# Another order of kept output blocks, the norm's squares in order, and value products in 64 columns, in a two-layer RG-LRU and attention kernel

## The chip, the cores and the metric

The kernel runs on one core of one Trainium2 chip. The metric is the device time of one execution in microseconds. The core's engines work side by side, each through its own queue in order: TensorE (PE in the profile, its weight loads PEld), VectorE (DVE), ScalarE (ACT), GpSimd (POOL) and SyncE (SP). POOL and SP do little but issue DMA transfers here. SBUF is the on-chip memory, PSUM the buffers that TensorE writes.

## What is computed

Two residual layers over one sequence of 1024 positions and 1024 channels, then a norm. The first mixes with a gated linear recurrence (width 1536, 12 blocks), the second with causal attention of 16 heads of 64 whose logits carry a forgetting term.

```python
def lru_mixer(h, ...):
    u = h @ w_in
    xb, gate = u[..., :1536], u[..., 1536:]
    xc = causal_depthwise_conv(xb, conv_w, conv_b)
    r = sigmoid(block_diag_linear(xc, wa, ba))
    i = sigmoid(block_diag_linear(xc, wx, bx))
    log_a = -8.0 * r * softplus(-a_param)
    a = exp(log_a)
    bterm = sqrt(-expm1(2.0 * log_a)) * (i * xc)
    hs = scan of h = a * h + bterm
    return (hs * silu(gate)) @ w_out

def fox_mixer(h, w_in, b_f, w_out):
    q, k, v, gate, f_logit = parts of h @ w_in
    cum = cumsum(log_sigmoid(f_logit + b_f))
    logits = q @ k.T / 8 + cum_q - cum_k, causal
    o = softmax(logits) @ v
    return (o * silu(gate)) @ w_out

x = x + lru_mixer(rms_norm(x), ...)
x = x + fox_mixer(rms_norm(x), ...)
out = rms_norm(x)
```

## The kernel before

Activations lie with the channels on the partitions, in two halves of 512 positions. Every product of the projections is made of two parts of each operand (`hi`, and `lo` = the rest), as three matmuls in a rounded 32-bit type: hi x hi, lo x hi, hi x lo (`gemm_steps`, line 128). `weights` (122) loads a weight block through a ring of tag `wf`, ScalarE makes `wh` and VectorE or GpSimd `wl`.

A scheduler places the instructions of each engine ahead of time by its own model of their durations. `tc.issue_after(i)` puts what stands in its block behind instruction `i` in the queue of `i`'s engine. All matmuls keep the order in which the program writes them, through `run` (853).

*First layer.* `split_x` and `square_x` (250, 261) make the two parts and the squares of x for one half; `square_x` adds seven of the eight squares into `acc` and keeps the last apart, so that `norm_row` (276) sums two tiles with matmuls against ones. The squares rotate through four buffers `sq`. `norm_row(0)` stands behind `square_x(1)`, which writes the same four buffers. `softplus` (213) works out constants of the recurrence; `conv(n)` (294), `gates`, `recur` and `outputs` follow for each of the 12 blocks.

*Between the layers* (lines 497 to 530) the last part of the output projection is added to x, x goes to DRAM as `x1d`, and `squares` and `rms_row` make the norm for each half: one tile of sums and, because of `wait`, the last square as a second tile; `inv_rms` (151) multiplies every tile with a column of ones, for four groups of 128 positions.

*Attention.* For each head, `maxima(hd, c)` (762) makes the scores `S` of four blocks of 128 queries in half c, VectorE masks them and takes the maximum, ScalarE the exponential. The weights become two f16 parts (`pp`: high in slot 0, low in slot 1) and a transposing DMA on SP turns them into `pT`. `weigh(hd, c)` (808) multiplies them with `v`, also two f16 parts of 64 columns each, side by side: one matmul against high and low of the weights for each block j of 128 keys, 8 in the first half of the positions and 16 in the second. O then holds in 64 partitions what the high part of v gives and in the other 64 what the low part gives, and lines 829 and 830 add the two. The parts of `v` lie in the order high of head 0, low of head 0, low of head 1, high of head 1.

`run` interleaves by hand: in an order string "1" is a step of the next scores, "0" a step of the products and "." a unit of the fill, six matmuls of the projections for later pairs of heads. `ORDER` (29) holds the strings for the first and the second half, `LAST` those of heads 12 on.

*Output.* From head 12 on the fill holds `partial` (912): for each of 8 blocks `db` of output channels and each half c, x1d is loaded by POOL, the product of the first six pairs of heads (`ops`, 18 matmuls in three steps) is added on VectorE (924) and the sum goes back to x1d by POOL (926). The order is (0, 0), (1, 0), (0, 1), (1, 1), (2, 0), (2, 1), (3, 0), (3, 1) and so on, as (db, c). Tiles come from a ring of two, tag `R`. Some blocks of half 0 are kept on chip instead (`kept`, line 919); their places come from `home` (902): two places in a buffer of tag `sg`, used until then for the gate of head pair 6, and four in the buffer `T0` of the keys, used until the scores of head 14 are done. `residual` (932) fetches the blocks that were not kept, on SP, into `U0` and the places that are left. `turned` (957) then transposes x, adds the last two pairs' products and does the final norm.

Of the kernel before, what the change touches and what calls it, by code (L numbers as in the profile page):

```python
# [19 lines left out]
P = 128  # L20
# [5 lines left out]
HD = 64  # L26
EPS = 1e-6
GROUP = 2
ORDER = "1.1..1.1..00", "1.1.1.1...0000"
LAST = "1..1..1..1..0.0", "1..1.1..1..0..0.0.0"  # L30
NEG = -1e30
PSUM = bass.MemoryType.PSUM
# [8 lines left out]
def trunk(ctx: ExitStack, tc: tile.TileContext, xt, w0, wg, wo0, pc, gn, gf, w1, wv, wf, bf, wo1, out):  # L41
# [17 lines left out]
    def matmul(*args, **kw):  # L59
        pe[0] = nc.tensor.matmul(*args, **kw)  # L60
        return pe[0]
# [126 lines left out]
    with ExitStack() as l0:  # L188
# [12 lines left out]
        def long(tag, dtype=F32, bufs=1):  # L201
            return tmp.tile([P, SEQ], dtype, tag=tag, name=tag, bufs=bufs)
# [54 lines left out]

        acc = long("m2")
        sq = [z[:, cs] for z in (long("th"), long("ti")) for cs in halves]

        def square_x(h):
            to = acc[:, halves[h]]
            sums[h].append(to)
            for k in range(KT):
                z = sq[k % 4] if k else to
                nc.scalar.activation(z, xs[h][k], AF.Square)
                if k == KT - 1:
                    sums[h].append(z)
                elif k:
                    nc.vector.tensor_tensor(to, to, z, ALU.add)  # L270
                yield
# [4 lines left out]
        def norm_row(h):  # L276

            row = ps.tile([P, HALF], F32, tag="O", name="rsrow")
            for i, sq_ in enumerate(sums[h]):
                matmul(row, onesf, sq_, start=i == 0, stop=i == len(sums[h]) - 1)  # L280
            r_ = rs[:, halves[h]]
            nc.scalar.activation(r_, row, AF.Sqrt, bias=epst, scale=1.0 / SEQ)
            return nc.vector.reciprocal(r_, r_)

        for _ in zip(split_x(0), square_x(0)):
            pass
# [122 lines left out]
        for n in range(NB):  # L409
            wu = first[0] if n == 0 else list(weights(w0[n]))  # L410
            if n == 1:
                ups = both = [ps.tile([P, HALF], F32, tag="g", name="ups") for h in range(2)]
            else:
                ups = two_banks("ups")
                both = [ups.rearrange("p a b -> p (a b)")]
                ups = [ups[:, h] for h in range(2)]
            product(ups[0], 0, wu)
            if n == 0:
                gps = held[0] = two_banks("gps")
                product(gps[:, 0], 0, first[1])  # L420
                for _ in zip(split_x(1), square_x(1)):
                    pass
                done = norm_row(0)
            else:
                gates(n - 1)
                if n > 1:
                    with tc.issue_after(state[n - 1]["last"].ins):
                        outputs(n - 2)
            product(ups[1], 1, wu)
            if n == 0:  # L430
                product(gps[:, 1], 1, first[1])
                norm_row(1)
                with tc.issue_after(done.ins):
                    softplus()
            conv(n, both)
            if n % 2 and n > 1:
                fill = itertools.chain(fill, project_out((n - 3) // 2))
            take(fill, 4)
            if n > 3:
                with tc.issue_after(state[n - 1]["last"].ins):  # L440
                    take(vsquares, 4)
            if n > 1:
                wn = list(weights(w0[NB + n - 1]))
                gps = held[n - 1] = two_banks("gps")
                for h in range(2):
                    product(gps[:, h], h, wn)
            if n:
                drain(silu(state[n - 1], held.pop(n - 1)))

                with tc.issue_after(state[n]["tap"].ins):  # L450
                    recur(n - 1)
            take(fill, 4)
# [45 lines left out]
        for h, cs in enumerate(halves):  # L498
            y = [tuple(z[:, cs] for z in p) for p in ys[-2:]]
            hT[h] = [pair() for k in range(KT)]  # L500
            parts = split_x(h, 1)
            sums = []
            for d0 in range(0, KT, 4):
                pts = []
                for db in range(d0, d0 + 4):
                    if db % 2 == 0:
                        two = ps.tile([P, 2, HALF], F32, tag="S", name="ops")
                    pts.append(two[:, db % 2])
                    mm3(pts[-1], wl[db][0], y[0], True, False)
                for db, o in enumerate(pts, d0):  # L510
                    mm3(o, wl[db][1], y[1], False, True)
                    x = xs[h][db]
                    nc.vector.tensor_tensor(x, x, o, ALU.add)  # L513
                    nc.sync.dma_start(x1d[h, :, db], x)
                    next(parts)
                    squares(
                        sums,
                        x,
                        lambda: nrm.tile([P, HALF], F32, tag="sq" if db else "ss", name="sq", bufs=2),
                        wait=db == KT - 1,  # L520
                    )
            rms_row(sums, rs1[h], rms1[h])
            if h == 0:
                value_bounds()
            nc.vector.tensor_tensor(
                rv[:, :, 4 * h : 4 * h + 4],
                rms1[h].unsqueeze(1).to_broadcast([P, 4, 4]),
                scale_v.unsqueeze(2).to_broadcast([P, 4, 4]),
                ALU.mult,
            )  # L530
# [7 lines left out]
    with ExitStack() as l1:  # L538
# [269 lines left out]
        def weigh(hd, c, sub=slice(0, HALF)):  # L808

            pair, s = hd // 2, hd % 2  # L810
            V, turned_ = Vs[pair], pT[c]
            if s == 0:
                yos[pair, c] = at.tile([P, HALF], F32, tag="yo", name="yo", bufs=2)
            yo = yos[pair, c][:, sub]
            begin, end = c * HALF + sub.start, c * HALF + sub.stop
            O = ps.tile([P, HALF], F32, tag="O", name="O")[:, : end - begin]
            nj = end // P
            for j in range(nj):
                v = V[j][:, 2 * s : 2 * s + 2].rearrange("p a d -> p (a d)")
                q = max(begin, j * P)  # L820
                for t in range(2):
                    p = turned_[:, j, t, q - c * HALF : end - c * HALF]
                    matmul(O[:, q - begin :], v, p, start=j == t == 0, stop=j == nj - 1 and t == 1)
                if j % 2 and j < nj - 1:
                    yield

            r0, r1 = s * HD, (1 - s) * HD
            to, one = yo[r0 : r0 + HD], unit_v[:, hd // 4 : hd // 4 + 1]
            nc.scalar.activation(to, O[r1 : r1 + HD], AF.Copy, scale=one[r1 : r1 + HD])
            nc.vector.scalar_tensor_tensor(to, O[r0 : r0 + HD], one[r0 : r0 + HD], to, ALU.mult, ALU.add)  # L830
            yield
# [69 lines left out]

        def home(db):

            if db == 3:
                two = at.tile([P, 2, HALF], F32, tag="sg", name="x3")
                homes[3], homes[2] = two[:, 0], two[:, 1]
            elif db == 5:
                four = tu.tile([P, 4, HALF], F32, tag="T0", name="x4")
                homes.update((4 + i, four[:, i]) for i in range(4))
            return homes[db]  # L910

        def partial(todo):

            for db, c in todo:
                split_out(db)
                if c if db < 2 else not c:
                    split_out(db + 1)

                kept = c == 0 and db in (3, 5, 6, 7)
                x = home(db) if kept else rpool.tile([P, HALF], F32, tag="R", name="xp")  # L920
                nc.gpsimd.dma_start(x, x1d[c, :, db])
                pt = ps.tile([P, HALF], F32, tag="g", name="ops1")
                yield from gemm_steps(pt, zip(wo[db], [y1[c][pair] for pair in range(6)]))
                nc.vector.tensor_tensor(x, x, pt, ALU.add)
                if not kept:
                    nc.gpsimd.dma_start(x1d[c, :, db], x)
# [5 lines left out]
        def residual(c, q):  # L932

            cs = slice(q * 256, (q + 1) * 256)
            if c == q == 0:
                two = tu.tile([P, 2, HALF], F32, tag="U0", name="x0")
                homes[0], homes[1] = two[:, 0], two[:, 1]
                for d in (0, 1, 2, 4):
                    fetch(homes[d], x1d[c, :, d])
            if c == 0:  # L940
                return [homes[d][:, cs] for d in range(KT)]
# [111 lines left out]
        for hd in range(HEADS):  # L1053
# [21 lines left out]
                    )  # L1075
            elif pair < 6:
                fill = chain(g_units(pair + 1), kq_units(pair + 2, ((1, (0,)),)))
            first, second = LAST if hd > 11 else ORDER
            if hd == HEADS - 1:
                first = "1..1.0.1.0.1..."  # L1080
            side = chain(pieces(hd + 1, 0, 0), pieces(hd + 1, 0, 1)) if hd else iter(())
# [105 lines left out]
```

## Time and profile before

| what | value |
|---|---|
| median of 3 runs | 1081.56 us (1079.12 to 1083.71) |
| the profiled execution | 1079.6 us |
| its span in the profile | 1077.8 us |
| mean granted TensorE clock | 0.995 |
| DMA moved | 142.55 MB |

The profile shows one execution. Busy times are per engine; a matmul's time is from its first column to its last result, so that successive matmuls overlap, and the distance between their starts tells what they take in a row. "f32" in a shape stands for four-byte elements, also the rounded type; "128*64" before a matmul's shape would be 128 active rows and 64 active columns of the array. A bracket at the end of a row of the order of time is the idle time of the engine before it and what ended it. Rows that an argument needs stand with it in the prediction.

### The profile page before, as it was taken

How to read it: one execution, taken by the hardware profiler on the slowest of the kernel's cores; microseconds unless marked ns; L12 is line 12 of the kernel's file. 1: busy time of each engine (PE TensorE's matmuls, PEld its weight loads, DVE VectorE, ACT ScalarE, POOL GpSimd, SP SyncE). 2: the span in 40 equal slices, each digit the busy share in tenths (PEclk: the TensorE clock that was granted, in tenths of full speed). 3: DMA queues.
4: the chain of work that ended last, by engine and by line, in shares of the span. 5: the costliest groups of instructions: out<-in, count | busy, mean ns of one | idle time of the engine just before them, and what ended most of it. 6: DMA issues, size and time to landing. Idle time of an engine off the chain costs nothing. (4 is left out here: it accounts for less than half of the span.)

```text
span 1077.8 us, 14962 instructions
## 1 busy us (share of the span) xinstructions
PE 1048.0 (97%) x5100; PEld 843.7 (78%) x5100; DVE 782.1 (73%) x1444; ACT 621.6 (58%) x1082; POOL 113.2 (11%) x91
## 2 busy tenths in 40 slices
PE   9999999999999999999999999999999999997997
PEld 7788888888888887797777797767977779765776
DVE  7889657766776589947878848788488866774665
ACT  8488453655465564745757636566466655653454
POOL 1322021202220210030000000000000000011200
PEclk9999999999999999999999999999999999998999
DMA  7111211222122112535878957899578885988994
GB/s 251 60 43 50 64 59 54 64 69 64 54 70 68 49 54 69 158 94 134 157 174 192 176 135 155 179 190 191 139 153 188 174 191 131 226 210 225 224 193 157
DMA packets 218508, 142.55 MB, mean 132 GB/s; under 512 B 161792, under 2 KB 178688, under 8 KB 218432
## 3 DMA queue, kind: packets, MB, share of 16 engines
q1 hardware_dynamic: 216032, 133.74, 52.3%
q0 software_dynamic: 2400, 7.87, 2.4%
q8 instruction: 40, 0.66, 0.3%
q14 instruction: 36, 0.29, 0.1%
HBM read 63.82 MB, written 14.81 MB: 73 GB/s over the span
## 5 line engine op out<-in xcount | busy, mean ns | idle before, releaser
L60 PE MATMUL gps<-hh,wh 128*128 128x512 f32 x576 | 227.3, 395 | 0.0
L60 PE MATMUL gps<-hh,wl 128*128 128x512 f32 x576 | 226.4, 393 | 0.8 <-DVE wl L101 0.7
L60 PE MATMUL gps<-hl,wh 128*128 128x512 f32 x576 | 226.6, 393 | 0.0
L90 ACT CAST wh<-wf 128x512 fp32r<-128x512 f32 (+2 forms) x162 | 97.3, 605 | 113.5 <-PE ops L60 43.0
L791 ACT ACTIVATE p<-S,m 128x128 f32<-128x128 f32 (+7 forms) x128 | 94.7, 740 | 67.6 <-DVE m L786 37.9
L101 POOL TENSOR_TENSOR wl<-wf,wh 128x512 fp32r<-128x512 f32 (+1 forms) x50 | 91.9, 1850 | 369.9 <-ACT wh L90 358.3
L60 PEld LDWEIGHTS gps<-hl,wh 128*128 128x128 f32 x576 | 108.4, 188 | 25.0 <-issue 0.5
L60 PEld LDWEIGHTS gps<-hh,wl 128*128 128x128 f32 x576 | 108.6, 189 | 22.5 <-DVE wl L101 1.0
L60 PEld LDWEIGHTS gps<-hh,wh 128*128 128x128 f32 x576 | 108.5, 188 | 21.6
L800 DVE SCALAR_TENSOR_TENSOR pp<-p,sums,pp 128x128 f16<-128x128 f32 (+7 forms) x128 | 103.1, 814 | 19.1 <-ACT pp L92 17.9
L92 ACT ACTIVATE pp<-p,sums 128x128 f16<-128x128 f32 (+7 forms) x128 | 95.5, 770 | 31.2 <-DVE sums L798 15.6
L786 DVE CUSTOM_DVE_ANT_0 S<-S,mask 128x128 f32<-128x128 f32 (+7 forms) x128 | 97.2, 760 | 16.9 <-PE S L60 15.6
L60 PE MATMUL S<-T,U 96*128 96x512 f32 (+7 forms) x384 | 94.3, 355 | 8.1 <-ACT p L791 8.0
L101 DVE TENSOR_TENSOR wl<-wf,wh 128x512 fp32r<-128x512 f32 x112 | 74.4, 668 | 25.8 <-ACT wh L90 25.6
L60 PEld LDWEIGHTS S<-T,U 128*128 128x128 f32 (+1 forms) x384 | 67.9, 190 | 26.2 <-ACT p L791 14.3
L389 DVE TENSOR_TENSOR x<-x,ops 128x512 f32<-128x512 f32 x80 | 54.1, 683 | 41.5 <-PE ops L60 41.4
L60 PE MATMUL ups<-hh,wh 128*128 128x512 f32 x192 | 75.6, 395 | 1.2 <-ACT hh L92 1.2
L60 PE MATMUL ups<-hl,wh 128*128 128x512 f32 x192 | 76.6, 399 | 0.2
L60 PE MATMUL ops<-yh,wl 128*128 128x512 f32 x192 | 75.7, 394 | 0.9 <-DVE wl L101 0.9
L60 PE MATMUL ops<-yh,wh 128*128 128x512 f32 x192 | 75.8, 396 | 0.5 <-DVE x L513 0.5
L60 PE MATMUL ups<-hh,wl 128*128 128x512 f32 x192 | 75.8, 395 | 0.0
L60 PE MATMUL O<-pT,v 128*128 128x512 f16 (+3 forms) x396 | 71.3, 322 | 3.8 <-DMA pT<-pp 3.6
(188 smaller groups left out, 1985.8 us busy)
## 6 DMA issues: line engine op xcount, KB each, us to landing
wf<-in_w SPq DMA_DIRECT2D x106, 256.0 KB
wf<-in_wo SPq DMA_DIRECT2D x64, 128.0 KB
T<-qkh SPq DMA_DIRECT2D x64, 128.0 KB
U<-qkh SPq DMA_DIRECT2D x64, 128.0 KB
x<-in_xt SPq DMA_DIRECT2D x16, 256.0 KB
wvf<-in_wv SPq DMA_DIRECT2D x32, 128.0 KB
x1d<-x SPq DMA_DIRECT2D x16, 256.0 KB
wf<-in_wv SPq DMA_DIRECT2D x16, 256.0 KB
```

Source lines behind the costliest of these rows:

```text
L60: pe[0] = nc.tensor.matmul(*args, **kw)
L90: nc.scalar.copy(hi, src)
L92: nc.scalar.activation(hi, src, AF.Copy, scale=scale)
L101: return eng.tensor_tensor(lo, src, f32(hi), ALU.subtract)
L389: nc.vector.tensor_tensor(x, x, pt, ALU.add)
L786: nc.vector.tensor_tensor_reduce(S[:, :n], S[:, :n], mask[:, SEQ - n :], -1.0, -NEG, ALU.add, ALU.min, accum_out=m)
L791: seen[0] = nc.scalar.activation(p, S[:, :n], AF.Exp, bias=m, scale=-1.0, accum_out=sums[:, i : i + 1])
L800: nc.vector.scalar_tensor_tensor(both[:, :, 1], p, r, both[:, :, 0], ALU.mult, ALU.subtract)
```

## The change

Four places are touched.

1. `kept` is half 0 of blocks 4 to 7 instead of 3, 5, 6 and 7. The `sg` buffer now holds blocks 4 and 3, the `T0` buffer blocks 2, 5, 6 and 7; blocks 0 to 3 are fetched back instead of 0, 1, 2 and 4.
2. In `weigh`, for the second half of a head in one piece (heads 0 to 14), the eight products with the weights' high parts come first. The eight with the low parts use only the 64 columns of v's high part (`V[j][:, 3 * s]`) and write to the lower or the upper 64 partitions of O, alternating, as the pairs of j and a in the loop say. The product of low with low is left out. The number of steps stays four.
3. Heads 2, 6 and 10 use another order string for the second half.
4. The last square of each half in the first layer has a buffer of its own (tag `sg`), the root in `norm_row` stands behind the latest square on ScalarE, `softplus` behind the last tap of the first convolution; between the layers, half 1 adds its last square to the sum instead of keeping it apart.

```diff
-ORDER = "1.1..1.1..00", "1.1.1.1...0000"
+ORDER = "1.1..1.1..00", ("1.1.1.1...0000", "1.1..1.1..0000")
...
+        sq_ = long("sg")
+        squared = [None]
...
-                z = sq[k % 4] if k else to
-                nc.scalar.activation(z, xs[h][k], AF.Square)
+                z = sq_[:, halves[h]] if k == KT - 1 else sq[k % 4] if k else to
+                squared[0] = nc.scalar.activation(z, xs[h][k], AF.Square)
...
-            nc.scalar.activation(r_, row, AF.Sqrt, bias=epst, scale=1.0 / SEQ)
-            return nc.vector.reciprocal(r_, r_)
+            with tc.issue_after(squared[0].ins):
+                nc.scalar.activation(r_, row, AF.Sqrt, bias=epst, scale=1.0 / SEQ)
+            nc.vector.reciprocal(r_, r_)
...
-                with tc.issue_after(done.ins):
-                    softplus()
-            conv(n, both)
+            conv(n, both)
+            if n == 0:
+                with tc.issue_after(state[0]["tap"].ins):
+                    softplus()
...
-                        wait=db == KT - 1,
+                        wait=h == 0 and db == KT - 1,
...
+            beside = c == 1 and sub.stop - sub.start == HALF
             for j in range(nj):
                 v = V[j][:, 2 * s : 2 * s + 2].rearrange("p a d -> p (a d)")
                 q = max(begin, j * P)
-                for t in range(2):
+                for t in range(1 if beside else 2):
                     p = turned_[:, j, t, q - c * HALF : end - c * HALF]
-                    matmul(O[:, q - begin :], v, p, start=j == t == 0, stop=j == nj - 1 and t == 1)
-                if j % 2 and j < nj - 1:
+                    matmul(O[:, q - begin :], v, p, start=j == t == 0, stop=not beside and j == nj - 1 and t == 1)
+                if j % 2 and j < nj - 1 and (j % 4 == 3 or not beside):
                     yield
+            if beside:
+                yield
+                for j, a in ((0, 0), (1, 1), (2, 0), (3, 1), (4, 0), (5, 1), (6, 1), (7, 0)):
+                    q = max(begin, j * P)
+                    matmul(
+                        O[a * HD : (a + 1) * HD, q - begin :],
+                        V[j][:, 3 * s],
+                        turned_[:, j, 1, q - c * HALF : end - c * HALF],
+                        start=False,
+                        stop=j > 5,
+                    )
+                    if j == 3:
+                        yield
...
-            if db == 3:
+            if db == 4:
                 two = at.tile([P, 2, HALF], F32, tag="sg", name="x3")
-                homes[3], homes[2] = two[:, 0], two[:, 1]
+                homes[4], homes[3] = two[:, 0], two[:, 1]
             elif db == 5:
                 four = tu.tile([P, 4, HALF], F32, tag="T0", name="x4")
-                homes.update((4 + i, four[:, i]) for i in range(4))
+                homes.update(zip((2, 5, 6, 7), (four[:, i] for i in range(4))))
...
-                kept = c == 0 and db in (3, 5, 6, 7)
+                kept = c == 0 and db > 3
...
-                for d in (0, 1, 2, 4):
+                for d in range(4):
...
-            first, second = LAST if hd > 11 else ORDER
+            first, second = LAST if hd > 11 else (ORDER[0], ORDER[1][hd % 4 == 2])
```

More of the change, by code (lines that the diff above doesn't have):

```diff
@@ L278, in norm_row @@
             row = ps.tile([P, HALF], F32, tag="O", name="rsrow")
-            for i, sq_ in enumerate(sums[h]):
-                matmul(row, onesf, sq_, start=i == 0, stop=i == len(sums[h]) - 1)
+            for i, z in enumerate(sums[h]):
+                matmul(row, onesf, z, start=i == 0, stop=i == len(sums[h]) - 1)
             r_ = rs[:, halves[h]]
-            nc.scalar.activation(r_, row, AF.Sqrt, bias=epst, scale=1.0 / SEQ)
-            return nc.vector.reciprocal(r_, r_)
+            with tc.issue_after(squared[0].ins):
+                nc.scalar.activation(r_, row, AF.Sqrt, bias=epst, scale=1.0 / SEQ)
+            nc.vector.reciprocal(r_, r_)
         for _ in zip(split_x(0), square_x(0)):
@@ L422, in trunk @@
                     pass
-                done = norm_row(0)
+                norm_row(0)
             else:
```

## The prediction

> **What bounds the kernel now.** I read the page's busy table first, then the windows by stage, then TensorE's order of time where it stands idle.
>
> ```profile
> span 1077.8 us, 14962 instructions
> PE 1048.0 (97%) x5100; PEld 843.7 (78%) x5100; DVE 782.1 (73%) x1444; ACT 621.6 (58%) x1082; POOL 113.2 (11%) x91
> 34.00:54.00 20.00, 20.00 (x87) 16.03 (x86) 19.89 (x27) 7.92 (x9) 4.54 (x4) 1.00 0.18 54
> 54.00:110.00 56.00, 56.00 (x244) 45.59 (x243) 50.05 (x52) 46.65 (x53) 13.84 (x6) 1.00 0.14 45
> 525.00:946.00 421.00, 410.81 (x2191) 329.38 (x2189) 310.69 (x745) 251.98 (x491) 1.24 (x2) 1.00 0.80 172
> 946.00:985.00 39.00, 37.74 (x171) 28.58 (x172) 24.50 (x60) 17.90 (x37) 6.47 (x12) 1.00 0.93 229
> 985.00:997.00 12.00, 6.48 (x19) 4.88 (x18) 6.73 (x17) 5.71 (x9) 1.62 (x3) 0.72 0.77 187
> 997.00:1036.00 39.00, 38.20 (x181) 29.06 (x180) 26.11 (x60) 19.06 (x36) 6.46 (x12) 1.00 1.07 222
> ```
>
> The window columns are stretch and length, then busy time of PE, PEld, DVE, ACT, POOL, then granted clock, DMA share and GB/s. TensorE sets the pace: 410.8 of 421 us busy in the attention stage. A matmul taken off it is worth about its own time there, as long as the next score block is not late. One stretch differs: 985 to 997 has 6.48 busy of 12 us and a granted clock of 0.72. In order of time:
>
> ```profile
> 984.27 1.08 PE L60 MATMUL S<-T,U 128*128 128x512 f32 x4 [0.31 <-ACT p L791]
> 990.87 0.80 PE L60 MATMUL ops<-yhh,wh 128*128 128x512 f32 x1 [5.52 <-DVE sums L797]
> 995.73 0.62 PE L60 MATMUL ops<-yhl,wh 128*128 128x512 f32 x1
> 996.16 1.13 PE L60 MATMUL S<-T,U 128*128 128x512 f32 x4
> 997.12 0.40 PE L60 MATMUL ops<-yhh,wh 128*128 128x512 f32 x1
> 999.68 0.40 PE L60 MATMUL ops<-yhl,wh 128*128 128x512 f32 x1
> 984.40 0.69 DVE L839 TENSOR_TENSOR yo<-yo,sg 128x512 f32<-128x512 f32 x1
> 990.13 0.69 DVE L924 TENSOR_TENSOR x<-x,ops 128x512 f32<-128x512 f32 x1 [2.93 <-DMA x<-x1d]
> 974.54 0.54 POOL L921 DMA_DIRECT2D xp<-x1d  x1 [3.56 <-DMA x1d<-xp]
> 981.32 0.54 POOL L921 DMA_DIRECT2D xp<-x1d  x1 [4.13 <-DMA x1d<-xp]
> 985.38 0.54 POOL L921 DMA_DIRECT2D x<-x1d  x1 [3.53 <-DVE sums L798]
> 985.38 4.72 DMA x<-x1d
> ```
>
> The first matmul of output block (4, half 0) starts after 5.52 us of idleness. It needs a PSUM buffer of tag g, which the add of block (3, half 0) at 990.13 gives free. That add waits for its x, whose load goes out only at 985.38: block 3 is a kept one, its home is a buffer of tag sg, and that is free only after the gating product of head 13 (984.40 on VectorE). The load then takes 4.72 us. Nothing else was late: the ordinary load behind it (974.54) had gone out 11 us earlier. The idleness also costs clock: the 12 matmuls from 990.87 to 996.16 start 0.441 us apart, the 12 from 997.12 on 0.233 us (11 steps to 999.68). So the place costs 5.52 + 12 x 0.208 = **8.0 us**.
>
> **1, another order of kept blocks.** Now (4, 0) is the kept block that takes the sg buffer, and (3, 0) an ordinary one in the ring R. In POOL's order (3, 0) takes the load slot of 974.54 that (3, 1) had, (3, 1) that of 981.32, and (3, 0) adds one store, while block 4 loses its store. Block 3 instead of 4 is fetched back on SP, and block 2's fetch moves to the T0 buffer, free after the last score block of head 14 (996.16). What is late next: (4, 0)'s load still goes out at 985.38 and lands at 990.10. Its product now runs from 985.2 (984.27 plus the 0.96 that separates 996.16 from 997.12): 18 matmuls at 0.233 and one score group of 0.96 give 990.4, so the add finds its x there, with 0.3 us to spare. (3, 1)'s x lands about 986.0; the buffer that its add frees is wanted at 990.4. Behind (4, 0)'s load POOL holds the store of (3, 1), whose add ends after 986 anyway. What can come back is DMA time: shares 0.93, 0.77, 1.07 over 39, 12 and 39 us make 87.2 us of 90. In 82 us, 5.2 would not fit if all of it were due there; the other end is nothing, since 1.07 counts overlapped packets. TensorE already waits once for such a transfer:
>
> ```profile
> 1014.47 1.04 PE L60 MATMUL O<-pT,v 128*128 128x512 f16 x4 [0.80 <-DMA pT<-pp]
> ```
>
> I take 1.7 back, nearer that 0.80 than 5.2. Part 1: **-6.3** (-8.0 to -2.8).
>
> **2, the low halves in 64 columns.** For the second half of heads 0 to 14 (the last head works in quarters and is unchanged) the eight products with the weights' low halves keep only v's high half. They go alternately to the upper and lower 64 PSUM partitions. The drop of one factor alone saves nothing, because a matmul's time goes by its moving columns:
>
> ```profile
> 567.09 2.99 PE L60 MATMUL O<-pT,v 128*128 128x512 f16 x16
> 569.88 0.84 PE L60 MATMUL S<-T,U 128*128 128x320 f32 x4
> L60 PE MATMUL O<-pT,v 128*128 128x512 f16 x182 | 45.7, 381 | 3.8 <-DMA pT<-pp 3.6
> L60 PE MATMUL O<-pT,v 128*128 128x128 f16 x66 | 9.1, 219 | 0.0
> L60 PEld LDWEIGHTS <-v 128*128 128x128 f16 x396 | 34.7, 98 | 42.6 <-issue 12.3 <-DMA pT<-pp 5.8 <-DMA U<-cumd 0.3
> L60 PEld LDWEIGHTS gps<-hh,wh 128*128 128x128 f32 x576 | 108.5, 188 | 21.6
> 476.68 0.29 PE L60 MATMUL vps<-wh,hh 128*128 128x272 f32 x1
> 476.81 0.27 PE L64 MATMUL fps<-ident,fz 128*16 128x128 f32 x1
> 476.83 0.37 PE L60 MATMUL vps<-wh,hl 128*128 128x272 f32 x1
> ```
>
> Sixteen products take 2.79 us (567.09 to 569.88). The slope of the two shapes is (381 - 219)/384 = 0.422 ns a column, with 165 ns fixed and overlapped. The low half has 5x512 + 384 + 256 + 128 = 3328 columns, 1.40 us, half of 2.79. Each of the two column groups now has 1664: if both stream at once the eight take 0.70 us, if they follow one another 1.40. No row shows two at once. I take 0.90: the 0.70, and two of the 98 ns loads left uncovered. Going over to a narrower array and back is bounded by nothing (the 16-column transpose at 476.81 is followed 0.02 us later, and it and its successor end 0.39 us after its start, with no gap beyond their columns) and by 0.165 + 0.098 = 0.26 us, a whole latency and a load in the open. I take 0.10, nearer the only row that shows a change of width. The eight stand together in heads 0 to 11 (two changes of width) and are cut by fill in 12 to 14 (four): 36 changes. 15 x 0.50 - 36 x 0.10 = 3.9 us. How much of it reaches the end: TensorE's waits from 540 to 920 us are these two (total, times, longest),
>
> ```profile
> PE S L60 <- ACT p L791: 6.3, 6, 2.1
> PE O L60 <- DMA pT<-pp: 2.8, 4, 1.4
> ```
>
> so in some heads the exponentials or the turned weights set the pace. The cover is partial, and I count three quarters: **-2.9** (-10.5 to +9.4, the ends being all overlapped with free changes, and none overlapped with each change at 0.26).
>
> On the loads, the Trainium skill, page "TensorE: Matmul & The Clock Gate", section "Weight-path perf modes", says that the fast load needs 128 columns and a type other than FP32; the trace agrees as far as it goes (f16 98 ns, f32 188 ns), and by that rule the 64-column loads would lose the fast form. By half of 188 ns they would not be longer than 98, and the sum would stay.
>
> **3, the second order string** for heads 2, 6 and 10 puts one fill unit more between their second and third score block and one less ahead of the products. It changes no work. Rows of heads 6 and 10:
>
> ```profile
> 711.76 0.50 PE L60 MATMUL S<-T,U 128*128 128x256 f32 x2 [0.60 <-ACT p L791]
> 715.28 0.62 PE L60 MATMUL S<-T,U 128*128 128x384 f32 x2 [1.62 <-ACT p L791]
> 841.85 0.62 PE L60 MATMUL S<-T,U 128*128 128x384 f32 x2 [1.07 <-ACT p L791]
> 848.82 2.99 PE L60 MATMUL O<-pT,v 128*128 128x512 f16 x16 [0.29 <-DMA pT<-pp]
> ```
>
> The waits of 0.60, 1.62 and 1.07 would go, 3.3 us, and the products would come earlier. But at 848.82 they already waited for the turned weights, so what is saved at the scores is lost there. Bounds -3.3 and +1.0 (a score block later, 1.07 on), I take **-0.5**.
>
> **4, squares and softplus.** The last square of the first layer gets a buffer of its own, and ScalarE's root goes behind the squares; softplus moves behind the first convolution. That is 17 VectorE operations of 0.17 us, 2.8 us, into a stretch where VectorE is 50.05 of 56 us busy; behind them wait the first gates' biases and the first recurrence on ScalarE, whose results TensorE needs only blocks later. TensorE is 20.00 of 20 and 56.00 of 56 us busy in the windows above: that work covers it, so 0 (a table load of 1.28 us bounds it either way, below). In the second layer's norm the last square of half 1 is added instead of multiplied:
>
> ```profile
> 463.45 1.62 PE L60 MATMUL sscol<-onesf,sq 128*128 128x1 f32 x14
> 464.13 1.57 DVE L553 MEMSET U<- 64x512 f32 x3 [1.40 <-DMA wf<-in_w]
> 17.63 1.28 ACT L215 ACT_TABLE_LOAD   x1
> ```
>
> Eight matmuls of 1.62/14 = 0.116 us go, 0.93, and one VectorE add of some 0.68 us comes, where VectorE waited 1.40 for a transfer. I take **-0.6** (-0.9 to +0.7).
>
> **Sum.** -6.3 - 2.9 - 0.5 - 0.6 = -10.3. The profiled execution took 1079.6 us (its span 1077.8 and 1.8 around it), so its like would take 1069.3. The median of the runs, 1081.56, lies 2.0 above it; from there the forecast is **1071 us**, with an own range of 1064 to 1077.
>
> **Rivals.** *Full overlap* (0.14): the two column groups stream at once, nothing of part 1 is given back, the order string keeps 2: -8.0 - 10.5 - 2 - 0.9 = -21.4, 1060. For it: the transpose row without a gap; against it: TensorE's waits for ScalarE. *No side by side* (0.10): the 64-column products follow one another at no extra cost and part 2 does nothing: -7.4, 1074. For it: no row shows two matmuls streaming at once. *The wait moves to the transfers* (0.13): the full 5.2 us of part 1 comes back at the products that wait for the turned weights, and part 2 keeps 0.4: -2.8 - 0.4 - 1.1 = -4.3, 1077. For it: DMA share 1.07; against it: only 0.80 us of such a wait there now. *The narrow mode drains the array* (0.13): each change of width waits out the 165 ns latency, and within the mode no load hides behind the running pair: 15 x 8 x 0.098 + 36 x 0.165 = +17.7, less 7.4 from the other parts, +10.3, **1092**. It decides from a loss of 7.4/15 = 0.49 us in each head's products. Against it: the transpose at 476.81; but that is one matmul of 16 columns between wide ones.
>
> The Trainium skill has that rule: "Mode switching requires drain" (page "TensorEngine Tiling (Array Packing)", section "Key Properties"), and the same page puts column tiling at the cost of the fast weight load; no run here shows either.
>
> **Chances and range.** Forecast 0.50, then 0.14, 0.10, 0.13, 0.13. About 0.5% (5.4 us) is what a measurement of this kernel can tell from no change. Faster than 1076.2: 0.48 + 0.14 + 0.07 + 0.05 = 0.74. Slower than 1087: 0.09 of the draining case's 0.13. Within: 0.17. The range 1062 to 1084 leaves out half of full overlap and most of the draining case.
>
> **What would show it.** Part 1: no idle above 1 us at the first matmul of block (4, 0) and a clock of 1.00 in that stretch; wrong if the wait sits at another add of the output or at the products. Part 2: the sixteen products of a head from first start to the next group's start in 2.5 us instead of 2.79; 2.1 means full overlap, 2.8 none, above 3.2 draining. Part 3: no wait at heads 6 and 10's third score block, and what the products then wait. Part 4: two matmuls of sscol for each column gone, TensorE still full from 34 to 110 us.

## The result, and the profile after

| | before | changed |
|---|---|---|
| median (lowest to highest) | 1082.05 us (1079.12 to 1083.71) | 1095.09 us (1094.36 to 1098.15) |
| span in the profile | 1077.8 us | 1092.6 us |

The column before has one run more than the table ahead of the prediction. The ratio is 1.0129 [1.0099, 1.0159]: 13 us slower, outside the predicted range. First the page of the changed kernel and its windows (columns as in the prediction).

```profile
span 1092.6 us, 14954 instructions
...
PE 1049.1 (96%) x5092; PEld 841.2 (77%) x5092; DVE 785.7 (72%) x1445; ACT 623.5 (57%) x1082; POOL 108.5 (10%) x91
```

```profile
54.00:110.00 56.00, 55.00 (x237) 44.03 (x236) 52.37 (x61) 44.99 (x52) 9.83 (x6) 1.00 0.15 45
525.00:946.00 421.00, 395.90 (x2115) 317.73 (x2114) 297.84 (x726) 241.90 (x472) 0.00 (x0) 0.97 0.75 161
...
985.00:1003.00 18.00, 18.00 (x86) 13.10 (x85) 7.46 (x15) 5.01 (x10) 2.83 (x6) 1.00 0.96 242
```

From 985 on, where before stood idle, TensorE is now full. The loss is in the attention stage: 395.9 busy of 421 us against 410.8 before, and a clock of 0.97. What TensorE waited for between 540 and 960 us, before and then after (total, times, longest):

```profile
PE S L60 <- ACT p L791: 6.9, 7, 2.1
PE O L60 <- DMA pT<-pp: 2.8, 4, 1.4
```

```profile
PE gps L60 <- ACT wh L90: 16.8, 3, 6.2
PE O L60 <- DMA pT<-pp: 5.2, 4, 2.1
PE vps L60 <- DVE sg L761: 2.7, 3, 0.9
```

A new wait is there three times, 16.8 us in all: the last 12 matmuls of the keys' projection (`gps`) wait for the rounded weights `wh`. The three places are heads 3, 7 and 11, where the values of the next four heads (`vps`) are worked out as well. The waits for the exponentials, 6.9 us before, are all but gone. TensorE in order of time, changed kernel:

```profile
617.13 0.39 PE L60 MATMUL vps<-wh,hh 128*128 128x256 f32 x1 [0.90 <-DVE sg L761]
...
627.25 0.79 PE L60 MATMUL gps<-hh,wh 128*128 128x512 f32 x1 [5.59 <-ACT wh L90]
...
630.27 0.55 PE L60 MATMUL gps<-hh,wh 128*128 128x512 f32 x1
...
631.82 2.40 PE L60 MATMUL O<-pT,v 128*128 128x512 f16 x16
...
759.41 0.79 PE L60 MATMUL gps<-hh,wh 128*128 128x512 f32 x1 [5.00 <-ACT wh L90]
...
763.28 0.60 PE L60 MATMUL gps<-hl,wh 128*128 128x512 f32 x1
...
893.79 0.79 PE L60 MATMUL gps<-hh,wh 128*128 128x512 f32 x1 [6.17 <-ACT wh L90]
...
899.38 1.85 PE L60 MATMUL O<-pT,v 128*128 128x512 f16 x6
```

After each stop the granted clock is down: 0.55 from 627 to 631 us, 0.50 from 759 to 763 and from 894 to 899.5. The 6 matmuls from 627.25 take 3.02 us where 6 x 0.23 = 1.38 is usual, the 8 from 759.41 take 3.87 for 1.84, the 12 from 893.79 take 5.59 for 2.76: 6.5 us more. With 16.8 and 2.7 of idleness that makes 26 us.

What `wh` waited for stands on ScalarE, and why that was late stands in SP's queue. Changed kernel, ScalarE and then SP:

```profile
626.58 0.62 ACT L90 CAST wh<-wf 128x512 fp32r<-128x512 f32 x1 [6.67 <-DMA wf<-in_w]
```

```profile
611.04 5.65 SPq L807 DMA_TRANSPOSE pT<-pp  x2
...
622.17 1.28 SPq L807 DMA_TRANSPOSE pT<-pp  x1
623.50 0.58 SPq L57 DMA_DIRECT2D wf<-in_w  x1
...
627.91 1.08 SPq L57 DMA_DIRECT2D wf<-in_wv  x2
```

and SP in the kernel before:

```profile
609.58 0.59 SPq L57 DMA_DIRECT2D wf<-in_w  x1
610.21 0.92 SPq L57 DMA_DIRECT2D wf<-in_wv  x2
611.24 7.88 SPq L802 DMA_TRANSPOSE pT<-pp  x2
```

Before, the second half of the keys' weights (`in_w`) and the last two of the four pieces of v's weights (`in_wv`) go out at 609.6 to 610.8, ahead of two transposes that hold the queue for 7.9 us while they wait for their data. In the changed kernel they stand behind these and three or four more transposes: the keys' load goes out at 623.50, the two of v's weights from 627.91 on. The stop at 627.25 is for the keys' load, since that cast (626.58) is the one that waits for `in_w`. No line of the change speaks of these loads. The scheduler, which plans every engine's queue by its own model of durations, has put them elsewhere.

### The profile page after: what moved, and what is told of

Read it like the earlier page. It is cut to its first block, busy times and chain, and to the rows that moved or that the text cites. A ratio compares the mean times of both kernels' runs of the same rounds, so it can differ in the third digit from the quotient of the medians.

```text
span 1092.6 us, 14954 instructions
## 1 busy us (share of the span) xinstructions
PE 1049.1 (96%) x5092; PEld 841.2 (77%) x5092; DVE 785.7 (72%) x1445; ACT 623.5 (57%) x1082; POOL 108.5 (10%) x91
## 5 line engine op out<-in xcount | busy, mean ns | idle before, releaser
L60 PE MATMUL gps<-hh,wh 128*128 128x512 f32 x576 | 230.0, 400 | 16.8 <-ACT wh L90 16.8
L60 PE MATMUL gps<-hh,wl 128*128 128x512 f32 x576 | 228.9, 397 | 0.9 <-DVE wl L101 0.7
L101 POOL TENSOR_TENSOR wl<-wf,wh 128x512 fp32r<-128x512 f32 (+1 forms) x50 | 87.3, 1755 | 376.8 <-ACT wh L90 376.8
L60 PE MATMUL vps<-wh,hh 128*128 128x256 f32 (+1 forms) x256 | 73.1, 287 | 2.7 <-DVE sg L761 2.7
```

The lines of the kernel that those rows point to most:

```text
L101: return eng.tensor_tensor(lo, src, f32(hi), ALU.subtract)
```

## The experiments

The runs were made in four groups, each beside its own runs of the kernel before. Those have medians from 1080.35 to 1081.93 us; the ratios are to them, and medians of different groups compare to within some 2 us.

**First: which part does it.** Theory A was that the narrow products and the new string together make the scheduler pull 36 of v's matmuls ahead of the last 12 of the keys' (617.13 above), and that this makes the loads late.

*e1, the changed kernel with the old string*

```diff
-first, second = LAST if hd > 11 else (ORDER[0], ORDER[1][hd % 4 == 2])
+first, second = LAST if hd > 11 else (ORDER[0], ORDER[1][0])
```

> The kernel after with the old order string in heads 2, 6 and 10; the narrow products, the kept blocks and the squares stay. Theory A (string and narrow products together made the scheduler put one weight load of heads 3, 7 and 11 behind five more transposes on SP, which cost 7.1 + 8.1 + 10.3 = 25.5 us in three stretches): the load is back in its place, 1095.1 - 25.5 = 1070 us, ratio to before 0.989, no idle above 2 us in those stretches. Rival B (the narrow mode itself costs): the sixteen products and the total stay as in the kernel after, 1095 us.

*e2, the changed kernel with 128 columns again*

```diff
-beside = c == 1 and sub.stop - sub.start == HALF
+beside = False
```

> The kernel after with the low halves at 128 columns as before; the new string, the kept blocks and the squares stay. Theory A: the late load goes as well, since it takes both parts, and the products lose 12 x 0.46 us and a little in heads 12 to 14: about 1076 us. Rival B: the same 1076 or less. Rival C (the string alone is the cause): still 1090 us or more.

*e3, the changed kernel with the value matmuls held behind the products, as in the program*

```diff
-                drain(vals)
+                with tc.issue_after(pe[0].ins):
+                    drain(vals)
```

> The kernel after with the value products of heads 3, 7 and 11 held on TensorE behind the last product of the head, as the kernel before has them; the weight load stays late on SP. Theory A (the late load is the cost): the wait at the two projection units stays and nothing fills it now, 1095 to 1105 us. Rival D (the value products that moved ahead are the cost): back to 1070 us.

*e4, the kernel before with part 1 alone* (the hunks in `home`, `partial` and `residual`)

> The kernel before with the new kept blocks alone. By the prediction's first part 6.3 us less, 1075.7, between 1074 and 1079, and no idle above 1 us at the first matmul of output block 4; if the transfers take it back, 1079.

e1 took 1093.04 us, ratio 1.0105 [1.0067, 1.0144]; e2 1096.08, 1.0145 [1.0105, 1.0185]; e3 1106.68, 1.0230 [1.0201, 1.0260]; e4 1076.39, 0.9947 [0.9927, 0.9966]. e4 gained what part 1 was to gain. e1 and e2 missed by 20 to 23 us: undoing either part alone doesn't help. They fall where their rivals had them (the narrow mode by itself, the string by itself), but both runs keep a stall at a weight load, and later runs rule these rivals out: with the loads on POOL, e7 and e16 have the 64 columns and e12 the string throughout, without the loss. In e1 the value matmuls are back in their place, and a wait nearly as long stands inside them, of `vps` for `wh`, 14.2 us in three times. e3 shows that pulling them ahead was no loss: held back, the wait for the keys' weights grows from 16.8 to 31.9 us in three times, and the time ends 1.7 us above the expected range. What e1, e2 and e3 have in common beside part 1, which e4 cleared, is part 4, so that was suspected next, against theory S: the place of a weight load in SP's queue, whichever part moves it.

**Second: part 4, or the queue.** *e5, the kernel before with part 4 alone* (the hunks in `square_x`, `norm_row`, `softplus` and `wait`)

> The kernel before with part 4 alone (squares, softplus, the norm's last square). Theory S: the loss comes from where the scheduler puts one weight load on SP, behind some fifteen transposes and pieces of keys, ahead of the value products of heads 3, 7 and 11; part 4 leaves SP's order there as in the kernel before, so 1079 to 1083 us. Rival P: part 4, which is in all three variants that lost there, upsets the attention stage: 1090 or more.

*e6, the kernel before with parts 1 and 2*

> The kernel before with parts 1 and 2 (kept order, 64 columns), without the string and the squares. Theory S: the fourth load of v's weights goes out behind the transposes, three stalls of 4 to 6 us in the value products at heads 3, 7 and 11, as in the run with the old string: 1088 to 1096 us. Rival P: without part 4 nothing of it: 1066 to 1074.

*e7, the changed kernel with the weight loads of heads 0 to 11 on POOL*

```diff
+wq = [None]
 def split_weights(src, shape, hi_eng, lo_eng, parts=wpool):
...
-            fetch(wt[:, :, sl], part)
+            (wq[0] or nc.sync).dma_start(wt[:, :, sl], part)
...
 for hd in range(HEADS):
+    wq[0] = nc.gpsimd if hd < 12 else None
```

> The changed kernel with all weight loads of heads 0 to 11 issued by POOL instead of SP, nothing else changed. Theory S: no load stands behind transposes any more; the 25 us lost around heads 3, 7 and 11 come back: 1066 to 1074 us. Rival: the load's place is a symptom and TensorE there is slow for another reason (clock, value products): 1088 or more.

*e8, the kernel before with the same edit*

> The kernel before with all weight loads of heads 0 to 11 issued by POOL. Control for the run beside it. Theory S: its loads were in time, so 1079 to 1084 us. Rival: POOL's queue is a gain by itself, 1075 or less, or a loss, 1087 or more.

e5 took 1080.03, 0.9991 [0.9971, 1.0010]; e6 1088.75, 1.0075 [1.0047, 1.0104]; **e7 1070.07, 0.9899 [0.9864, 0.9933]**; e8 1081.59, 1.0015 [0.9994, 1.0037]. All four as theory S had it. Part 4 alone costs and brings nothing, and e6, without it, has the stalls. POOL's queue is no gain by itself, but it takes 25 us off the changed kernel. In e7 the three late loads of head 3 go out between 592.6 and 609.9, those of v's weights when `wl`, a reader of the ring's buffers, is done:

```profile
592.60 0.54 POOL L116 DMA_DIRECT2D wf<-in_w  x1 [9.72 <-DVE pp L807]
595.60 0.54 POOL L116 DMA_DIRECT2D wf<-in_wv  x1 [2.46 <-DVE wl L101]
609.86 0.54 POOL L116 DMA_DIRECT2D wf<-in_wv  x1 [13.73 <-DVE wl L101]
```

The traces give the times at which the keys' load and the last piece of v's weights for head 3's group are issued in each run:

| run | parts | keys' load issued | last v piece issued | TensorE's wait for `wh` at gps and vps, 3 places | median |
|---|---|---|---|---|---|
| before | none | 609.58 | 610.75 | none | 1082.05 |
| e4 | 1 | 610.26 | 611.44 | none | 1076.39 |
| e5 | 4 | 611.06 | 612.25 | none | 1080.03 |
| e6 | 1, 2 | 609.38 | 628.53 | 13.8, vps | 1088.75 |
| e1 | 1, 2, 4 | 611.24 | 629.75 | 14.2, vps | 1093.04 |
| e2 | 1, 3, 4 | 612.56 | 631.24 | 8.6, vps | 1096.08 |
| changed | all | 623.50 | 628.55 | 16.8, gps | 1095.09 |
| e7 | all, POOL | 592.60 | 609.86 | none | 1070.07 |

With part 1 or 4 alone the loads stay; in each run that has part 2 or part 3 and loads on SP the last piece of v's weights goes out 18 to 20 us later. With parts 2 and 3 together the keys' load is 14 us late as well, and there TensorE's stops are for that one. No run with loads on SP has part 2 or 3 alone, or parts 1 and 4 without them.

**Third: is one load enough, and what are the parts worth without it.** *e9, e6 with only the last piece of v's weights on POOL*

```diff
-            fetch(wt[:, :, sl], part)
+            (nc.gpsimd if last else nc.sync).dma_start(wt[:, :, sl], part)
...
-                parts += split_weights(src, (2, 256 + ex), nc.scalar, nc.gpsimd if ex else nc.vector)
+                parts += split_weights(src, (2, 256 + ex), nc.scalar, nc.gpsimd if ex else nc.vector, last=not ex and k == 6)
```

> Parts 1 and 2 as in the run of both, with one thing more: the last of the four loads of v's weights (three loads in the whole program) is issued by POOL, all others stay on SP. Theory S, in its narrowest form: those three loads are the loss, so the stalls of 4.2, 5.1 and 5.0 us in the value products go, with the slow clock behind them: 1070 to 1075 us against 1088.75. Rival Q: SP's queue as a whole is too full in the changed program and another load or transpose takes their place: 1083 or more.

*e10, e7 with the edit of e2*

> The changed kernel with POOL's loads, and the low halves in 128 columns again: what part 2 is worth when no load is late. By the prediction's term 2.9 us more than the 1070.07 with part 2: 1073. If all that the products save (0.46 us in each of 15 heads) reached the end: 1077. If waits for the turned weights eat it: 1070.

*e11, e7 with the edit of e1*

> The changed kernel with POOL's loads and the old string for heads 2, 6 and 10: what part 3 is worth when no load is late. By the prediction's term 0.5 us more than 1070.07: 1070.6. If its three waits at the score blocks all came back: 1073.4. If the string only moves the wait to the products: 1070 or less.

*e12, e7 with the new string for heads 0 to 11* (`ORDER[1][1]`)

> The changed kernel with POOL's loads and the new string for the second half of all heads 0 to 11: a trial for a better version. If score blocks are what is late in the other heads too, 1067 to 1069; if the products, which come one fill unit earlier, then wait for the turned weights, 1070 to 1076.

e9 took 1079.10, 0.9983 [0.9964, 1.0002]: 9.7 us of the 14 to 19 that theory S in its narrowest form asked for. The stalls in the value matmuls are gone, but ScalarE now waits at the cast of the keys' weights, which SP issued at 609.4 and which landed at about 614.7. Its place is not the cause: e6 issued it at the same time and cast at 612.89, so here it landed 1.9 us later, with the piece that POOL issued at 608.65 under way beside it. That the two slow each other fits these times, and was not tried. ScalarE works in order and the exponentials of the next score block stand behind that cast; so TensorE's score blocks wait in turn (ScalarE, then TensorE's waits from 540 to 960 us):

```profile
614.76 0.62 ACT L90 CAST wh<-wf 128x512 fp32r<-128x512 f32 x1 [3.97 <-DMA wf<-in_w]
615.28 0.47 ACT L791 ACTIVATE p<-S,m 128x256 f32<-128x256 f32 x1
```

```profile
PE S L60 <- ACT p L791: 12.1, 7, 2.8
```

e10 took 1078.72, 0.9982 [0.9959, 1.0005], so part 2 is worth 8.6 us where no load is late, above all three figures that were expected. e11 took 1071.99, 0.9925 [0.9898, 0.9951]: the string is worth 1.9, which its interval doesn't tell from nothing. e12 took 1068.67, 0.9893 [0.9869, 0.9916], the lowest of all, and not told from e7.

**Fourth: the converse, and which loads.** *e13, the kernel before with the last piece of v's weights put where e6 has it*

```diff
         for part, sl in src:
-            fetch(wt[:, :, sl], part)
+            with tc.issue_after(behind) if behind else ExitStack():
+                fetch(wt[:, :, sl], part)
...
+                    behind=turns[-1].ins if k == 6 and not ex else None)
```

> The kernel before with one thing changed: the last of the four loads of v's weights for heads 3, 7 and 11 is put on SP behind the latest transpose of the next head's first half, the place that it has in the run of parts 1 and 2. Theory S: this place alone makes the stall in the value products, 4 to 6 us of idleness and about 1.5 of slow clock three times: 1094 to 1100 us. Rival: it needs the shorter products of part 2 to become late, and here it stays under 1086.

*e14, the changed kernel with only v's weights on POOL* (`queue=nc.gpsimd` in `values` alone)

> The changed kernel with only the loads of v's weights on POOL; those for keys, queries and gates stay on SP. If the fourth load of v's weights were all of it: 1070. If, as the run with one load showed, ScalarE's cast of the keys' weights then waits for its load (about 3 us and slow clock in heads 3, 7 and 11): 1077 to 1083.

*e15, the reverse: keys', queries' and gates' weights on POOL, v's on SP*

> The changed kernel with only the loads of the keys', queries' and gates' weights on POOL, v's weights on SP, where the fourth load still stands behind the transposes. Theory: both kinds of load are late one by one, so the stall in the value products is there: 1083 to 1093. Rival: the load for the keys was all of it, 1070 to 1074.

*e16, the kernel before with POOL's loads and part 2 alone*

> The kernel before with POOL's loads and part 2 alone: what the 64 columns are worth without a late load and without the other parts, against 1081.59 for POOL's loads alone. The prediction's term: 2.9 less, 1078.7. What the products save by the trace (0.46 us in each of 15 heads), if all reaches the end: 7 less, 1074.7. As much as between the two runs that differ in part 2 alone (8.6): 1073.

e13 took 1097.54, 1.0167 [1.0124, 1.0210]. **One load of 256 KB, three times in the program, put later in SP's queue by an edit that does nothing else, costs the kernel before 16.8 us**, more than the whole change lost. SP, ScalarE and TensorE of e13:

```profile
610.66 0.43 SPq L57 DMA_DIRECT2D wf<-in_wv  x1
...
628.96 0.43 SPq L57 DMA_DIRECT2D wf<-in_wv  x1
```

```profile
634.11 0.62 ACT L90 CAST wh<-wf 128x512 fp32r<-128x512 f32 x1 [9.48 <-DMA wf<-in_wv]
```

```profile
634.78 0.38 PE L60 MATMUL vps<-wh,hh 128*128 128x256 f32 x1 [3.84 <-ACT wh L90]
...
635.99 0.42 PE L60 MATMUL vps<-wh,hh 128*128 128x256 f32 x1
...
639.20 0.33 PE L60 MATMUL vps<-wh,hh 128*128 128x256 f32 x1
639.37 0.28 PE L60 MATMUL vps<-wh,hl 128*128 128x256 f32 x1
639.49 0.28 PE L60 MATMUL vps<-wl,hh 128*128 128x256 f32 x1
```

The chain: issued 628.96, cast begun 634.11, matmul 634.78 after 3.84 us of idleness, then 15 matmuls from 635.99 to 639.20 at 0.214 us apart where 0.12 (639.37 to 639.49) is usual, 1.4 us more. Three times 5.2 is 16.

e14 took 1072.12, 0.9927 [0.9900, 0.9954]: with v's weights alone off SP nearly all comes back, though the keys' weights stay there. But the scheduler placed the keys' load anew, at 612.38 instead of 623.50, ahead of the two transposes as in the kernel before (SP of e14):

```profile
612.38 0.54 SPq L116 DMA_DIRECT2D wf<-in_w  x1
```

So e14 took both kinds of late load away, and doesn't tell which of them the changed kernel paid for. The cast that held up e9 no longer does, so e9's loss hangs on the other pieces of v's weights that it left on SP, or on the parts it lacked; that was not taken apart. e15 took 1105.50, 1.0230 [1.0187, 1.0272], above both figures that were expected and worse than the changed kernel. Its keys' load is early (592.68 on POOL), but its last two pieces of v's weights go out at 633 (SP, then TensorE's waits):

```profile
633.12 0.94 SPq L116 DMA_DIRECT2D wf<-in_wv  x2
```

```profile
PE vps L60 <- ACT wh L90: 22.4, 3, 7.7
```

So late pieces of v's weights are dear by themselves (e13, e15). What the keys' load alone costs, the one that stops TensorE in the changed kernel, no run shows. e16 took 1073.60, 0.9932 [0.9909, 0.9955]: part 2 is worth 8.0 us against e8.

## Why the prediction was wrong, step by step

**The step that failed** is the way in which parts 2 and 3 were made into a sum. Part 2 was priced as "15 x 0.50 - 36 x 0.10 = 3.9 us", three quarters of it counted, and of part 3 it was said that "it changes no work". Both took the rest of each queue as it stood in the profile of before. But the scheduler places all engines' work by modelled durations, so parts 2 and 3 also change the order on SP, where neither has a line. The runs show in its place weight loads put behind transposes in each group of values. One of them, the last piece of v's weights 18 us later, costs 16.8 us by itself (e13). In the changed kernel there are three, the keys' load 14 us late and two of v's weights, and with all of them on POOL 25.0 us come back (1095.09 to 1070.07). No term, bound or rival held a moved load. That the time came near the 1092 of the draining case is chance, since that case's sign, products above 3.2 us, isn't there. The description of the kernel was wrong in the same place: not all matmuls keep the program's order, since those of the values stand outside `run`. Nothing in the profile of before says that the order would change. What it does say is how little room there was: the three loads at 609.6 to 610.8 stand just ahead of two transposes that hold SP for 7.88 us.

**Part 1** was right. The block (4, 0) starts without a gap in the changed kernel, and e4 gained 5.5 us by its medians, 1081.93 to 1076.39, where 6.3 were forecast. What came back came where it was said, at the products that wait for turned weights, and was larger in e4's profile than the 1.7 taken: 4.89 against 0.80 before, 4.1 of the 5.2 that bounded it. TensorE of the changed kernel and of e4:

```profile
1002.95 0.40 PE L60 MATMUL ops<-yhh,wh 128*128 128x512 f32 x1
...
1028.46 1.04 PE L60 MATMUL O<-pT,v 128*128 128x512 f16 x4 [1.03 <-DMA pT<-pp]
```

```profile
1008.31 1.89 PE L60 MATMUL O<-pT,v 128*128 128x512 f16 x4 [4.89 <-DMA pT<-pp]
```

**Part 2** had the right mechanism and too small a size. The changed kernel's products of head 1: TensorE, the last wide product and the first two narrow ones by themselves, the weight loads, and the group of the narrow loads:

```profile
567.93 2.40 PE L60 MATMUL O<-pT,v 128*128 128x512 f16 x16
570.26 0.86 PE L60 MATMUL S<-T,U 128*128 128x320 f32 x4
```

```profile
569.29 0.22 PE L60 MATMUL O<-pT,v 128*128 128x128 f16 x1
```

```profile
569.44 0.41 PE L60 MATMUL O<-pT,v 128*64 128x512 f16 x2
```

```profile
567.92 1.35 PEld L60 LDWEIGHTS <-v 128*128 128x128 f16 x8 [0.26 <-issue]
569.44 0.57 PEld L60 LDWEIGHTS <-v 128*64 128x64 f16 x8 [0.16 <-issue]
```

```profile
L60 PEld LDWEIGHTS <-v 128*64 128x64 f16 x120 | 5.2, 109 | 6.5 <-issue 4.1
```

Sixteen take 2.33 us (567.93 to 570.26) against 2.79; 2.5 was forecast. The narrow eight take 0.82 (569.44 to 570.26), of which one column group's 1664 columns at 0.422 ns are 0.70. Both groups stream at once: two start at 569.44, two at 569.68. A change of width costs about 0.1 us: the last wide product's 128 columns, 0.054 us from 569.29, are through at 569.34, 0.095 before the first narrow one, and the last narrow columns are through 0.095 before 570.26. The forecast had 0.10 for it. What it had too large was the two weight loads left uncovered, 0.20 in each head: the narrow columns are through in 0.73 (0.82 less 0.095), only 0.03 above the 0.70.

So "no side by side" and "the narrow mode drains the array" fell, since two changes at the latter's 0.165 and eight loads in the open would make the sixteen longer than 3.2 us. The Trainium skill has "Mode switching requires drain" (page "TensorEngine Tiling (Array Packing)", section "Key Properties"); this trace agrees in that 0.095 us pass at each change, and doesn't show whether the array empties in them. On the loads, the Trainium skill's page "TensorE: Matmul & The Clock Gate", section "Weight-path perf modes", would take the fast form from the 64-column loads; this trace agrees as far as it goes, since a load of half the columns takes 109 ns and not less than 98. Most of that lies beside the running pairs.

The rest of the size is the factor of three quarters. Where no load is late part 2 is worth 8.0 (e8 to e16) and 8.6 us (e10 to e7). The products save 0.46 in each of heads 0 to 11 and 0.16 in heads 12 to 14 (2.32 to 2.16 in e8 and e16, where fill cuts them), 6.0 in all; the intervals, 3 to 4 us either way for a difference of two runs, hold that. In their profiles the waits that were to eat a quarter of it did not grow. TensorE's waits from 540 to 960 us, e8 and then e16:

```profile
PE S L60 <- ACT p L793: 6.0, 5, 2.0
...
PE S L60 <- DMA U<-qkl: 1.1, 1, 1.1
PE O L60 <- issue: 1.1, 1, 1.1
...
PE O L60 <- DMA pT<-pp: 1.0, 2, 0.8
```

```profile
PE O L60 <- DMA pT<-pp: 3.8, 4, 2.0
PE S L60 <- DMA U<-qkl: 2.8, 3, 1.5
PE S L60 <- ACT p L793: 2.3, 3, 0.8
```

They moved from the exponentials to the transfers, 9.2 us before and 8.9 after.

**Part 3** alone, without late loads, brought 1.9 us, not told from the 0.5 forecast. Its waits at the score blocks go (2.5 us for the exponentials in e11's attention stage, none in e7's). **Part 4** was costed at -0.6, and e5 can't tell it from nothing. TensorE was busy for 55.00 of 56 us from 54 on, 55.02 in e5: the moved constants, 20 operations on VectorE and not 17, make the first gates wait 0.8 us for VectorE, where the forecast had 0. **The sum** of the four, -10.3, is -11.5 where no load is late (e8 1081.59 to e7 1070.07). That 1070.07 lies so near the 1071 forecast is luck in part: measured one by one the parts make some 16 us (5.5, 8.0 to 8.6, 1.9, 0.3), which the intervals don't tell from 11.5, and part 2 is more than double its term.

What stays open is why the scheduler's model moves these loads when products get shorter or steps are shifted, and which of the late loads cost how much in the changed kernel. The moves were seen in the order on SP run by run, and not followed into the model. Nor was it tried to keep the loads on SP and pin their place there.

## What to carry to other kernels

Where a scheduler orders the queues, an edit on one engine can re-order another's. Before pricing the edit, look for loads that stand on a shared queue just ahead of instructions that wait long, and count what each costs if it falls behind them. Loads whose lateness stops an in-order engine belong on a queue that holds nothing that waits for something else: here POOL's, which does nothing from 525 to 946 us in the changed kernel. The loads there cost the kernel before nothing that its interval shows, and gained the changed one 25 us. And when several variants lose the same amount in the same place, compare the order of issue between those that lose and those that don't, before suspecting the part they have in common.

## What the runs showed of the hardware

Two products in the two halves of the array's columns do run side by side: eight take 0.82 us with 3328 columns in all, which one after the other would be 1.40. Going from 128 columns to 64 and going back cost 0.095 us each. A stop of 3.8 to 6.2 us costs another 1.4 to 2.8 us in slow matmuls, which is 0.3 to 0.5 of the idleness, and goes into the price of a late load.
